# adaLN's four later vectors in a fused encoder layer: from scaled additions over rows of inputs to multiply-and-sum over rows of features, spread over units 7 to 103

## The chip, the cores and the metric

One NeuronCore of a Trainium2 chip runs the whole layer. The metric is the device time of one execution in microseconds, the median of several runs. Engines are named as in the profile: PE multiplies matrices, PEld loads its weights, DVE (VectorE) and ACT (ScalarE) work element by element and read PSUM, POOL (GpSimd) works on SBUF alone, and SP issues nearly all DMAs, in the order of its queue.

## What is computed

Batch 1, 1024 tokens, width 1024, all in fp32. The part that the change concerns is the modulation, six vectors of 1024 from the conditioning vector c:

```python
c_act = jax.nn.silu(c)
mod = c_act @ w_ada + b_ada          # (1, 6*1024), w_ada is 1024 x 6144
shift_mix, scale_mix, gate_mix, shift_ffn, scale_ffn, gate_ffn = jnp.split(mod, N_MOD, axis=-1)

h = modulate(rms_norm(x), shift_mix, scale_mix)
proj = h @ w_in                      # q, k, v of 8 + 8 heads
...                                  # chunked attention, stick-breaking attention
mixed = jnp.concatenate([rms_norm(oa) * g_a, rms_norm(ob) * g_b], axis=-1) @ w_out
x = x + gate_mix[:, None, :] * mixed
h = modulate(rms_norm(x), shift_ffn, scale_ffn)
gate, val = jnp.split(causal_depthwise_conv(h @ w_up, conv_w, conv_b), 2, axis=-1)
x = x + gate_ffn[:, None, :] * ((jax.nn.silu(gate) * val) @ w_down)
return rms_norm(x) * final_g
```

The first two vectors are needed before any projection; the other four only later: `gate_mix` when the output projection is scaled, `shift_ffn` and `scale_ffn` after attention, `gate_ffn` in the feed-forward part.

## The kernel before, in words

Matrix products in fp32 are made of three passes over values split in a high and a low part (`mm3g`), so PE has three matmuls for each product and DVE, ACT and POOL have the splitting.

**Stages.** (1) Norm, the first two modulation vectors and the first head pair's q and k, up to about 70 us of the trace. The two vectors are made here by `ada_sum` (L250): the weights lie with features on partitions, silu(c) is spread over all partitions in the tile `cbc`, and one `tensor_tensor_reduce` (L254) multiplies 1024 inputs and adds them up. (2) Attention, to about 640 us. (3) The rest of the output projection and the second norm. (4) The feed-forward blocks, to the end. The change acts in stage 2.

**Attention.** A loop (L943) runs over 128 units: 8 head pairs of 16 units, the first four pairs stick-breaking (units 0 to 63), the last four chunked attention (units 64 to 127). A pass of the loop computes the scores of the unit two ahead, transposes the weights of the present unit, and multiplies by the values every second unit (`pv`). For a stick-breaking unit the weights need a scan on DVE (L799, tile `kt`), then a product on POOL (L802, tile `pb`), then PE's transposes (`T<-ident,pb`), a copy on ACT (`pth`) and the low part on DVE (`ptl`, L822). For a chunked unit they need a maximum on DVE (L767 to L776, tile `nm`), ACT's exponential (L778, `pb`), and a scaling on POOL (L795). Between these, `fill` deals out a quota of projection matmuls (jobs: q and k of later pairs, v, and at the end `job_out_b`, the first part of the output projection, L545, and `job_out_a`, L581). `job_out_b` loads `gate_mix` into a tile `kt` (L560) and scales its results on DVE (L567, tile `wl`). Its weights are loaded as `raw`, copied on DVE (L521) and POOL (L522) to tiles `H`.

**Order.** PE's instructions are kept in the order in which they are written (`pe`, L135), and so is any instruction wrapped in `ko`. The others, DVE's in attention among them, are placed by a scheduler; SP's DMAs too. Every engine then runs its queue in order: an instruction that waits holds all that stand behind it.

**The four later vectors** (`mods`, L891) are a generator that the loop advances once per unit from unit 60 (`MOD0`, L971). Two tiles of 128 inputs by 256 features (`rawm`, 128 KB, 4 buffers) are handled per step: DVE multiplies each by the input's silu(c) and adds it to a sum `macc` (L916 the first, L918 the other seven of eight). After eight tiles `mod_out` (L923) adds over partitions on PE, with a column of ones (two matmuls `T<-ones,macc`) for `shift_ffn` and `scale_ffn`, or with a matrix of ones (`T<-macc,ones`) for the two gates; DVE adds the bias (L930, L936) and a gate's row goes to DRAM (`gate_d`).

```python
            if kb == 0:
                ...
                acc = mk(p1, [P, QC], F32, "macc")
                ve.tensor_scalar(acc, w, cact[:, 0:1], None, ALU.mult)
            else:
                ve.scalar_tensor_tensor(acc, w, cact[:, kb:kb + 1], acc, ALU.mult, ALU.add)
            if kb == KB - 1:
                mod_out(i, qt, acc, cols)
```

Of the kernel before, what the change touches and what calls it, by code (L numbers as in the profile page):

```python
# [11 lines left out]
F32 = mybir.dt.float32  # L12
F32R = mybir.dt.float32r
AF = mybir.ActivationFunctionType
ALU = mybir.AluOpType
# [4 lines left out]
P = 128  # L20
S = 1024
D = 1024
KB = D // P
TB = S // P
HALF = 512
# [9 lines left out]
NEG = -1.0e30  # L35
# [11 lines left out]
T2A, T2B = 6, 2  # L47
MOD0 = 60
FILL = 2, 2, 0, 0
MODS = 2, 3, 4, 5  # L50
# [5 lines left out]
def build(nc, tc, t, ctx):  # L56
    sy, ve, sc, gp, te = nc.sync, nc.vector, nc.scalar, nc.gpsimd, nc.tensor
    cnt = [0]

    def mk(pool, shape, dt, tag):  # L60
        cnt[0] += 1
        return pool.tile(shape, dt, name=f"{tag}_{cnt[0]}", tag=tag, bufs=BUFS.get(tag, 1))
# [8 lines left out]
    f = lambda ap: ap.bitcast(F32)  # L71


    _, dr = pool("dr", space=DRAM)
# [3 lines left out]
    gate_d = mk(dr, [2, D], F32, "gated")  # L78
    rev_d = mk(dr, [8, P, ULEN], F32, "revd")

    c0, p0 = pool("p0", side="left")
# [12 lines left out]
    bada = sm[:, 16:64]  # L94
# [40 lines left out]
    def pe(fn, *a, **k):  # L135
        r = fn(*a, **k)  # L136
        return tc.keep_in_program_order(r) if pin[0] else r
# [4 lines left out]
    lo64, hi64 = slice(0, HD), slice(HD, P)  # L142
    smask = mk(pq, [P, P], F32, "smask")
    gp.memset(smask, 0.0)
    gp.affine_select(out=smask, in_=smask, pattern=[[-1, P]], compare_op=ALU.is_gt,
                     fill=NEG, base=0, channel_multiplier=1)
    smaskr, identr = (mk(pq, [P, P], F32R, n) for n in ("smaskr", "identr"))
    gp.tensor_copy(smaskr, smask)
    gp.tensor_copy(identr, ident)
# [62 lines left out]
    def new_k(pr):  # L212
        pr.kh = [mk(pq, [P, S], F32R, "kh") for _ in range(2)]
# [3 lines left out]
    cs, pst = pool("pst", side="right", reuse_waits="tile")  # L217
    ada = t["ada0"]
    sh_mix = mk(p0, [P, KB], F32, "sh_mix")
    sc_mix = mk(p0, [P, KB], F32, "sc_mix")  # L220
# [233 lines left out]
    split_v0(1)  # L454
    sy.dma_start(rev_d, bass.AP(t["rev"].tensor, 0, [[ULEN, 8], [0, P], [1, ULEN]]))
    new_k(pairs[0])
    for hf in range(2):
# [84 lines left out]
    def load_gate(dst):  # L542
        sy.dma_start(dst, bass.AP(gate_d.tensor, gate_d.offset, [[0, P], [1, D]]))

    def job_out_b(_):  # L545
# [8 lines left out]
        for fb in fbs:  # L554
            wo[fb, 1] = load_wout(fb, 1)
        bc = mk(p1, [P, S + 1], F32, "kt")
        load_gate(bc[:, 0:D])
        gate.append(bc)
# [329 lines left out]

    QC = 256

    def mods():  # L891


        seq = [(i, qt, kb) for i in MODS for qt in range(D // QC) for kb in range(KB)]
        tiles = {}

        def load(n):
            if n < len(seq):
                i, qt, kb = seq[n]
                tiles[n] = mk(p1, [P, QC], F32, "rawm")  # L900
                sy.dma_start(tiles[n], t["ada"][i - 2, kb, :, qt * QC:(qt + 1) * QC])

        load(0)
        load(1)
        yield
        for n, (i, qt, kb) in enumerate(seq):
            cols = i in (3, 4)
            if n % 2 == 0:
                load(n + 2)
                load(n + 3)  # L910
            w = tiles.pop(n)
            if kb == 0:
                if cols and qt == 0:
                    modv[i] = mk(p0, [P, KB], F32, f"mod{i}")
                acc = mk(p1, [P, QC], F32, "macc")
                ve.tensor_scalar(acc, w, cact[:, 0:1], None, ALU.mult)  # L916
            else:
                ve.scalar_tensor_tensor(acc, w, cact[:, kb:kb + 1], acc, ALU.mult, ALU.add)  # L918
            if kb == KB - 1:
                mod_out(i, qt, acc, cols)  # L920
            if n % 2:
                yield

    def mod_out(i, qt, acc, cols):
        mp = mk(ps1, [P, HALF], F32, "T")
        if cols:
            for b in range(2):
                pe(te.matmul, mp[:, b:b + 1], acc[:, b * P:(b + 1) * P], ones[:, 0:1], start=True, stop=True)
            k0 = 2 * qt
            ve.scalar_tensor_tensor(modv[i][:, k0:k0 + 2], mp[:, 0:2], 0.0 if i == 3 else 1.0,  # L930
                                    bada[:, 8 * i + k0:8 * i + k0 + 2], ALU.add, ALU.add)
        else:
            pe(te.matmul, mp[:, 0:QC], ones, acc, start=True, stop=True)
            bb = mk(p1, [1, QC], F32, "rawm")
            sy.dma_start(bb, bass.AP(t["b_ada"].tensor, i * D + qt * QC, [[QC, 1], [1, QC]]))
            ve.tensor_add(acc[0:1], mp[0:1, 0:QC], bb)  # L936
            sy.dma_start(gate_d[i // 5:i // 5 + 1, qt * QC:(qt + 1) * QC], acc[0:1])

# [5 lines left out]
    for i in range(-AHEAD, len(units) + 1):  # L944
# [23 lines left out]
        for x in later:  # L968
            x[0] -= 1
            if x[0] == 0:  # L970
                x[1]()  # L971
        if i >= MOD0:
            next(bg, None)
# [547 lines left out]
```

## Time and profile before

| | us |
|---|---|
| median of three runs (1423.1 to 1428.0) | 1426.03 |
| the profiled execution | 1425.51 |
| its span, first to last instruction | 1423.5 |
| busy: PE, DVE, POOL, ACT | 1309.2, 1176.2, 864.9, 617.2 |

The span is what the instructions cover; the execution's own time is 2.0 us longer. Busy times are sums over stages that are limited by different things, so a term is read in its stage: the view by stretches gives the busy time of each engine there, the granted clock of PE (1.00 is full speed, 0.5 half) and the DMA share; the view of waits tells who waited for whom.

### The profile page before, as it was taken

How to read it: one execution, taken by the hardware profiler on the slowest of the kernel's cores; microseconds unless marked ns; L12 is line 12 of the kernel's file. 1: busy time of each engine (PE TensorE's matmuls, PEld its weight loads, DVE VectorE, ACT ScalarE, POOL GpSimd, SP SyncE). 2: the span in 40 equal slices, each digit the busy share in tenths (PEclk: the TensorE clock that was granted, in tenths of full speed). 3: DMA queues.
4: the chain of work that ended last, by engine and by line, in shares of the span. 5: the costliest groups of instructions: out<-in, count | busy, mean ns of one | idle time of the engine just before them, and what ended most of it. 6: DMA issues, size and time to landing. Idle time of an engine off the chain costs nothing.

```text
span 1423.5 us, 19845 instructions
## 1 busy us (share of the span) xinstructions
PE 1309.2 (92%) x6644; PEld 1083.0 (76%) x6644; DVE 1176.2 (83%) x1967; ACT 617.2 (43%) x1270; POOL 864.9 (61%) x760
## 2 busy tenths in 40 slices
PE   4889999999899978798887999999999999999996
PEld 2688998898778966676665877777777778777774
DVE  7858777677778868876889889999998889899887
ACT  5647567575545433333432333323333333333334
POOL 4646576765333436563578667776676677667664
PEclk9999999999999999899998999999999999999998
DMA  8534433414665686665011111111111111211213
GB/s 311 180 100 112 104 88 85 119 49 120 166 167 144 179 263 197 217 193 193 22 45 36 47 52 45 45 45 60 52 54 58 45 45 45 60 52 49 62 37 119
DMA packets 80047, 144.57 MB, mean 102 GB/s; under 512 B 10041, under 2 KB 36809, under 8 KB 79946
## 3 DMA queue, kind: packets, MB, share of 16 engines
q1 hardware_dynamic: 79946, 143.31, 33.9%
q8 instruction: 53, 0.87, 0.3%
q14 instruction: 48, 0.39, 0.1%
HBM read 102.89 MB, written 18.88 MB: 86 GB/s over the span
## 4 chain that ended last, share of the span: by engine, by line
PE 43%; DVE 35%; ACT 7%; issue 5%; DMA 5%; POOL 4%; SPq 1%; POOLq 0%; DVEq 0%; ACTq 0%
PE mm L136 14%; PE up L1128 12%; DVE y L1137 8%; PE T L136 6%; PE dnf L136 6%; DVE x L1262 4%; PE S L136 3%; ACT y L1133 3%; DVE ah L1071 3%; DVE y L1070 2%; DVE adaw L254 1%; DVE macc L918 1%; PE up L1302 1%; POOL wl L121 1%; DVE al L1072 1%
## 5 line engine op out<-in xcount | busy, mean ns | idle before, releaser
L1262 DVE TENSOR_TENSOR x<-dnf,x 128x512 f32<-128x512 f32 x340 | 222.5, 679 | 1.6 <-PE dnf L136 1.6
L1137 DVE SCALAR_TENSOR_TENSOR y<-y,sm,y 128x512 f32<-128x512 f32 (+2 forms) x160 | 187.3, 1171 | 28.8 <-ACT y L1133 28.7
L1128 PE MATMUL up<-h,wh 128*128 128x512 f32 x640 | 199.7, 393 | 2.6 <-ACT y L1170 1.8
L1094 POOL TENSOR_TENSOR wl<-raw,wh 128x1024 fp32r<-128x1024 f32 (+1 forms) x62 | 160.1, 2583 | 66.1 <-ACT wh L1092 59.5
L1133 ACT ACTIVATE y<-y,sm 128x512 f32<-128x512 f32 x80 | 65.3, 817 | 254.7 <-DVE y L1209 133.4
L136 PE MATMUL mm<-H,wh 128*128 128x512 f32 x448 | 150.2, 403 | 0.0
L1128 PEld LDWEIGHTS up<-h,wh 128*128 128x128 f32 x640 | 119.7, 189 | 31.1 <-ACT y L1170 5.2
L136 PE MATMUL dnf<-dh,ah 128*128 128x512 f32 x336 | 133.5, 397 | 10.0 <-DVE x L1262 8.8
L136 PE MATMUL dnf<-dl,ah 128*128 128x512 f32 x336 | 134.0, 399 | 3.7 <-POOL dl L1240 2.5
L802 POOL TENSOR_TENSOR pb<-pb,kt 128x512 f32<-128x512 f32 (+2 forms) x96 | 89.4, 945 | 77.0 <-DVE kt L799 50.0
L136 PE MATMUL dnf<-dh,al 128*128 128x512 f32 x336 | 132.6, 395 | 0.9 <-DVE al L1072 0.9
L1128 PE MATMUL up<-h,wl 128*128 128x512 f32 x320 | 125.3, 392 | 0.0
L822 DVE TENSOR_TENSOR ptl<-T,pth 128x512 fp32r<-128x512 f32 (+2 forms) x192 | 98.5, 517 | 30.7 <-ACT pth L821 29.0
L821 ACT CAST pth<-T 128x512 fp32r<-128x512 f32 (+2 forms) x192 | 87.4, 457 | 62.3 <-PE T L136 60.9
L795 POOL TENSOR_SCALAR pb<-pb,ri 128x640 f32<-128x640 f32 (+2 forms) x64 | 45.4, 711 | 106.2 <-DVE ri L794 67.7
L136 PE MATMUL mm<-wh,H 128*128 128x256 f32 x512 | 102.8, 292 | 6.6 <-DVE vs L511 6.6
L799 DVE TENSOR_TENSOR_SCAN kt<-kt 128x128 f32<-128x128 f32 (+3 forms) x64 | 98.2, 1534 | 9.8 <-ACT kt L784 9.4
L1128 PE MATMUL up<-Tc,wh 128*128 128x512 f32 x320 | 100.9, 396 | 4.6 <-ACT y L1154 4.5
L1240 POOL TENSOR_TENSOR dl<-modt,dh 128x512 fp32r<-128x512 f32 x42 | 65.3, 1554 | 64.3 <-ACT dh L1239 64.3
L1237 POOL TENSOR_TENSOR modt<-modt,modt 128x512 f32<-128x512 f32 x44 | 68.8, 1563 | 58.2 <-DMA modt<-w_down 58.2
L136 PE MATMUL S<-kh,qs 128*128 128x384 f32 (+5 forms) x352 | 99.5, 364 | 4.6 <-ACT pb L778 4.4
L136 PE MATMUL T<-ident,pb 128*128 128x128 f32 x528 | 91.1, 277 | 8.8 <-POOL pb L802 3.5
(214 smaller groups left out, 3451.1 us busy)
## 6 DMA issues: line engine op xcount, KB each, us to landing
raw<-w_up SPq DMA_DIRECT2D x44, 512.0 KB, 3.6
rawm<-ada SPq DMA_DIRECT2D x128, 128.0 KB, 2.4
qs<-ex SPq DMA_DIRECT2D x104, 128.0 KB, 2.5
modt<-w_down SPq DMA_DIRECT2D x44, 256.0 KB, 2.7
adaw<-ada SPq DMA_DIRECT2D x16, 512.0 KB, 5.7
raw<-w_qk SPq DMA_DIRECT2D x16, 512.0 KB, 3.6
kh<-ex SPq DMA_DIRECT2D x56, 128.0 KB, 2.6
tbd<-wh SPq DMA_DIRECT2D x18, 256.0 KB, 2.6
```

The lines of the kernel that those rows point to most:

```text
L136: r = fn(*a, **k)
L799: ve.tensor_tensor_scan(r, r, r, 1.0, ALU.mult, ALU.bypass)
L802: gp.tensor_mul(pt[:, a:b], pt[:, a:b], kt[:, a + 1:b + 1])
L821: sc.copy(dh, tp[:, 0:b - a])
L822: ve.tensor_sub(dl, tp[:, 0:b - a], f(dh))
L1094: late.append(lambda a=a, z=z: ko(gp.tensor_sub(wl[:, a:z], raw[:, a:z], f(wh[:, a:z]))))
L1128: ko(te.matmul(ps, w[x][:, kb], b[kb][y], start=start and n == 0, stop=n == 11, skip_group_check=True))
L1133: ko(sc.activation(y[:, a:z], src[:, a:z], AF.Identity, scale=cw[2][:, b], bias=cb[:, b]))
L1137: ko(ve.scalar_tensor_tensor(y[:, o:z], src[:, o - d:z - d], cw[2 - d][:, b], y[:, o:z], ALU.mult, ALU.add))
L1237: ko(gp.tensor_mul(raw, raw, gbc[hf]))
L1240: ko(gp.tensor_sub(wl, raw, f(wh)))
L1262: r = ve.tensor_add(xc, ps, xc)
```

## The change

The four later vectors are made the way `ada_sum` makes the first two. The host hands over the weights transposed, features on partitions. silu(c), which stage 1 has spread over the partitions, is saved in DRAM (`c_d`) and read back spread over 128 partitions, half of it (512 inputs) at a time, into `chalf`. One `tensor_tensor_reduce` on DVE (`ISA rawm,asum` and a second instruction that reads the accumulator) handles 128 features by 512 inputs (`rawm`, now 256 KB, 2 buffers). There are 64 of them: 2 halves, 4 vectors, 8 blocks. They are pinned in order (`ko`). The sum is complete without PE; two small DVE operations add the halves and the bias; a gate is written to DRAM from 128 partitions, element by element. The generator now starts at unit 7 (the first from 6 on that is no multiple of 3) and moves one tile a step, in two units of three, so that the last sum is written at unit 103. `job_out_b` and `job_out_a` are as before, but `job_out_b` first makes sure that the first gate has been issued. The mask `smask` moves to a pool that is closed after stage 1.

```diff
-    "pb": 3, ..., "rawm": 4, ...
+    "pb": 3, ..., "rawm": 2, ...
-MOD0 = 60
+MOD0 = 6
+    c_d = mk(dr, [1, D], F32, "cd")
     sy.dma_start(rev_d, bass.AP(t["rev"].tensor, 0, [[ULEN, 8], [0, P], [1, ULEN]]))
+    sy.dma_start(c_d, cbc[0:1])
         bc = mk(p1, [P, S + 1], F32, "kt")
+        while not gate_up:
+            next(bg)
         load_gate(bc[:, 0:D])
-    QC = 256
+    asum = mk(p0, [P, 2, len(MODS), KB], F32, "asum")
+    gate_up = []
     def mods():
-        seq = [(i, qt, kb) for i in MODS for qt in range(D // QC) for kb in range(KB)]
...
+        seq = [(hf, n, kb) for hf in range(2) for n in range(len(MODS)) for kb in range(KB)]
+        tiles, ch = {}, {}
+        def load(x):
+            if x < len(seq):
+                hf, n, kb = seq[x]
+                cc = slice(hf * HALF, (hf + 1) * HALF)
+                if n == 0 and kb == 0:
+                    ch[hf] = mk(p1, [P, HALF], F32, "chalf")
+                    sy.dma_start(ch[hf], bass.AP(c_d.tensor, c_d.offset + hf * HALF, [[0, P], [1, HALF]]))
+                tiles[x] = mk(p1, [P, HALF], F32, "rawm")
+                sy.dma_start(tiles[x], t["ada"][n, kb, :, cc])
         load(0)
-        load(1)
         yield
...
+        for x, (hf, n, kb) in enumerate(seq):
+            load(x + 1)
+            w = tiles.pop(x)
+            ko(ve.tensor_tensor_reduce(out=w, in0=w, in1=ch[hf], scale=1.0, scalar=0.0, op0=ALU.mult, op1=ALU.add,
+                                       accum_out=asum[:, hf, n, kb:kb + 1]))
+            if hf and kb == KB - 1:
+                mod_out(n, MODS[n])
+            yield
+    def mod_out(n, i):
+        v = modv[i] = mk(p0, [P, KB], F32, f"mod{i}")
+        ve.tensor_add(v, asum[:, 0, n], asum[:, 1, n])
+        ve.scalar_tensor_tensor(v, v, 1.0 if i == 4 else 0.0, bada[:, 8 * i:8 * i + KB], ALU.add, ALU.add)
+        if i in (2, 5):
+            sy.dma_start(bass.AP(gate_d.tensor, gate_d.offset + i // 5 * D, [[1, P], [P, KB]]), v)
+            gate_up.append(i)
-        if i >= MOD0:
+        if i >= MOD0 and i % 3:
             next(bg, None)
-    ada = w6[:, :, 2:6].transpose(2, 0, 1, 3)
+    ada = w_ada[0].T.reshape(6, KB, P, D)[2:6]
```

What it does to the queues, at three places. Line numbers of the changed program are 1 to 4 off those of before (L803 is L799, L826 is L822, L851 is L847, L523 is L521).

DVE in the large units of the first stick-breaking pair, before (`kt` the scans, `ptl` the low parts, `ex` a projection's low part):

```order
L847 TENSOR_TENSOR o_1244<-T_1246,fx_1245 64x256
L822 TENSOR_TENSOR ptl_1264<-T_1261,pth_1263 128x128
L822 TENSOR_TENSOR ptl_1228<-T_1279,pth_1227 128x4x128
L799 SCALAR_TENSOR_TENSOR kt_1271<-kt_1271 128x1024
L160 SCALAR_TENSOR_TENSOR ex_1299<-mm_1146,ex_1298 128x512
L822 TENSOR_TENSOR ptl_1264<-T_1314,pth_1263 128x2x128
L822 TENSOR_TENSOR ptl_1339<-T_1333,pth_1338 128x4x128
```

and after:

```order
L851 TENSOR_TENSOR o_1254<-T_1256,fx_1255 64x256
L826 TENSOR_TENSOR ptl_1274<-T_1271,pth_1273 128x128
L917 ISA rawm_1180,asum_581<-rawm_1180,chalf_1099 128x512
L917 ISA asum_581 128x1
L826 TENSOR_TENSOR ptl_1238<-T_1292,pth_1237 128x4x128
L803 SCALAR_TENSOR_TENSOR kt_1284<-kt_1284 128x1024
L156 SCALAR_TENSOR_TENSOR ex_1312<-mm_1153,ex_1311 128x512
L826 TENSOR_TENSOR ptl_1274<-T_1327,pth_1273 128x2x128
L917 ISA rawm_1277,asum_581<-rawm_1277,chalf_1099 128x512
L917 ISA asum_581 128x1
L826 TENSOR_TENSOR ptl_1355<-T_1349,pth_1354 128x4x128
```

Two sums stand where none stood, each ahead of a low part that PE's value products read. 35 of the 64 sums stand ahead of the last stick-breaking scan, and all 64 ahead of the instructions that the trace of before shows from 505 us on.

DVE near the end of attention, while `job_out_b` runs, before:

```order
L521 CAST H_7672<-raw_7670 128x512
L918 SCALAR_TENSOR_TENSOR macc_7483<-rawm_7598,cact_76,macc_7483 128x256
L793 TENSOR_TENSOR rs_7609<-rs_7609 128x1
L847 TENSOR_TENSOR o_7530<-T_7688,fx_7687 64x256
L794 RECIPROCAL ri_7633<-rs_7609 128x1
L521 CAST H_7678<-raw_7676 128x512
L822 TENSOR_TENSOR ptl_7711<-T_7708,pth_7710 128x128
L855 SCALAR_TENSOR_TENSOR otl_7700<-o_7530,sm_74,oth_7699 128x256
L918 SCALAR_TENSOR_TENSOR macc_7483<-rawm_7600,cact_76,macc_7483 128x256
L764 MEMSET S_7726 64x64
```

and after:

```order
L523 CAST H_7448<-raw_7446 128x512
L797 TENSOR_TENSOR rs_7379<-rs_7379 128x1
L851 TENSOR_TENSOR o_7312<-T_7458,fx_7457 64x256
L798 RECIPROCAL ri_7403<-rs_7379 128x1
L826 TENSOR_TENSOR ptl_7481<-T_7478,pth_7480 128x128
L768 MEMSET S_7484 64x64
L859 SCALAR_TENSOR_TENSOR otl_7470<-o_7312,sm_75,oth_7469 128x256
```

The two additions to `macc` are gone, and nothing of the later vectors stands here any more.

PE at the same place, before:

```order
L136 MATMUL T_7688<-ptl_7511,vs_5290 128x128
L136 MATMUL T_7708<-ident_65,pb_7489 128x128
L136 MATMUL T_7720<-macc_7483,ones_70 128x256
L136 MATMUL S_7726<-kh_6270,vs_6714 128x384 x2
L136 MATMUL mm_7682<-H_6785,H_6768 128x512
```

and after:

```order
L137 MATMUL T_7458<-ptl_7293,vs_5285 128x128
L137 MATMUL T_7478<-ident_66,pb_7271 128x128
L137 MATMUL S_7484<-kh_6187,vs_6587 128x384 x2
L137 MATMUL mm_7452<-H_6658,H_6641 128x512
```

The matmul on `macc` is gone from between a transpose and the scores. There were 24 such matmuls (8 for the gates, 16 for the two columns) and none is left; PE's order is otherwise the same. On SP 128 loads of `rawm`, 8 of the bias and 8 gate rows become 64 loads, two of `chalf`, one write of `c_d` and two gates.

## Rows read from the trace of the kernel before

**Rows 1.** The page: busy time by engine, share of the span, instructions.
```profile
PE 1309.2 (92%) x6644; PEld 1083.0 (76%) x6644; DVE 1176.2 (83%) x1967; ACT 617.2 (43%) x1270; POOL 864.9 (61%) x760
```

**Rows 2.** Stretches of attention: length, busy us (instructions) by engine, clock, DMA share, GB/s.
```profile
core 0: us, PE busy (x) PEld busy (x) DVE busy (x) ACT busy (x) POOL busy (x), PEclk, DMA share, GB/s
100.00:340.00 240.00, 234.82 (x1542) 212.25 (x1542) 180.66 (x257) 159.01 (x377) 162.54 (x227) 0.99 0.37 94
340.00:505.00 165.00, 156.21 (x994) 139.18 (x993) 133.34 (x446) 84.44 (x242) 62.11 (x89) 0.98 0.60 164
505.00:640.00 135.00, 110.53 (x578) 90.08 (x577) 107.33 (x281) 45.02 (x133) 74.31 (x76) 0.92 0.70 216
```

**Rows 3.** The same stretches, instructions on the tile macc alone (PE, PEld, DVE).
```profile
340.00:505.00 165.00, 5.76 (x32) 4.45 (x32) 43.81 (x84) 0.98 0.60 164
505.00:640.00 135.00, 4.71 (x16) 2.70 (x16) 29.64 (x44) 0.92 0.70 216
```

**Rows 4.** PE's waits from 345 to 480 us: total, times, longest.
```profile
PE S L136 <- ACT pb L778: 4.4, 4, 2.3
PE T L136 <- DVE macc L918: 3.1, 1, 3.1
```

**Rows 5.** PE's waits from 480 to 630 us.
```profile
PE T L136 <- DVE macc L918: 8.8, 2, 6.6
PE mm L136 <- DVE H L521: 6.1, 2, 3.6
PE S L136 <- ACT pb L778: 2.2, 1, 2.2
```

**Rows 6.** PE in order of time: start, duration, instruction, idle before.
```profile
343.20 0.65 PE L136 MATMUL T<-macc,ones 128*128 128x256 f32 x2
343.50 0.58 PE L136 MATMUL S<-kh,qs 128*128 128x256 f32 x2
...
600.31 1.19 PE L136 MATMUL T<-macc,ones 128*128 128x256 f32 x2 [6.59 <-DVE macc L918]
```

**Rows 7.** DVE in order of time, 593 to 601 us.
```profile
598.69 1.48 DVE L918 SCALAR_TENSOR_TENSOR macc<-rawm,cact,macc 128x256 f32<-128x256 f32 x1
```

**Rows 8.** Stretches that hold the waits on macc, columns as in rows 2.
```profile
405.00:420.00 15.00, 11.95 (x60) 9.95 (x59) 9.34 (x30) 4.90 (x16) 2.82 (x5) 0.89 0.67 178
545.00:560.00 15.00, 9.88 (x54) 7.57 (x53) 13.22 (x36) 4.20 (x15) 8.58 (x12) 0.97 0.69 226
595.00:610.00 15.00, 9.69 (x47) 8.33 (x48) 11.08 (x26) 2.97 (x8) 7.28 (x7) 0.77 0.52 164
```

**Rows 9.** Groups by line on DVE: count, ns min/median/max; then busy, mean ns, idle.
```profile
L254 DVE CUSTOM_DVE_ANT_0 adaw<-adaw,cbc x16: 1209/1212/2309, 18.2 to 55.4; 128x1024 f32<-128x1024 f32 x16
L771 DVE CUSTOM_DVE_ANT_0 S<-S,kt x64: 285/432/433, 332.9 to 626.8; 128x256 f32<-128x256 f32 x56, 128x128 f32<-128x128 f32 x8
L254 DVE DVE_READ_ACCUMULATOR2_ANT sh_mix<- x8: 76/78/83, 19.3 to 55.0; 128x1 f32 x8
L918 DVE SCALAR_TENSOR_TENSOR macc<-rawm,cact,macc x112: 414/485/1594, 76.9 to 620.0; 128x256 f32<-128x256 f32 x112
...
L918 DVE SCALAR_TENSOR_TENSOR macc<-rawm,cact,macc 128x256 f32<-128x256 f32 x112 | 66.9, 597 | 9.0 <-DMA rawm<-ada 8.0
```

**Rows 10.** Fullest stretches of DVE in stick-breaking, columns as in rows 2.
```profile
130.00:140.00 10.00, 10.00 (x62) 8.70 (x61) 9.02 (x10) 7.90 (x18) 5.58 (x10) 1.00 0.52 124
240.00:250.00 10.00, 10.00 (x64) 8.92 (x64) 9.01 (x11) 8.21 (x20) 8.50 (x12) 1.00 0.36 83
```

**Rows 11.** PE's waits from 70 to 345 us.
```profile
PE T L136 <- POOL pb L802: 3.5, 3, 1.6
PE T L136 <- DVE ptl L822: 1.7, 1, 1.7
```

**Rows 12.** DMA issues by line: count, KB each, median us to landing.
```profile
modt<-w_down SPq DMA_DIRECT2D x44, 256.0 KB, 2.7
```

More of the change, by code (lines that the diff above doesn't have):

```diff
@@ L142, in build @@
     lo64, hi64 = slice(0, HD), slice(HD, P)
[L143 to L146, printed above, removed]
     smaskr, identr = (mk(pq, [P, P], F32R, n) for n in ("smaskr", "identr"))
-    gp.tensor_copy(smaskr, smask)
     gp.tensor_copy(identr, ident)
@@ L218, in build @@
     ada = t["ada0"]
+    smask = mk(pst, [P, P], F32, "smask")
+    gp.memset(smask, 0.0)
+    gp.affine_select(out=smask, in_=smask, pattern=[[-1, P]], compare_op=ALU.is_gt,
+                     fill=NEG, base=0, channel_multiplier=1)
+    gp.tensor_copy(smaskr, smask)
     sh_mix = mk(p0, [P, KB], F32, "sh_mix")
@@ L887, in build @@
     modv = {}
-    QC = 256
+    asum = mk(p0, [P, 2, len(MODS), KB], F32, "asum")
+    gate_up = []
     def mods():
-        seq = [(i, qt, kb) for i in MODS for qt in range(D // QC) for kb in range(KB)]
[L895 to L901, printed above, removed]
+        seq = [(hf, n, kb) for hf in range(2) for n in range(len(MODS)) for kb in range(KB)]
[9 more added lines that the diff above has]
+                sy.dma_start(tiles[x], t["ada"][n, kb, :, cc])
@@ L903, in mods @@
         load(0)
-        load(1)
         yield
[L906 to L937, printed above, removed]
+        for x, (hf, n, kb) in enumerate(seq):
[6 more added lines that the diff above has]
+            yield
```

2 rows, old and new, of the table BUFS are left out of this document.

## The prediction

> **What bounds the kernel now.** I read the page first, then the attention stage in stretches, then PE's waits there, then PE and DVE in order of time at the longest of them. The page says that PE is busy for 92% of the span and DVE for 83% [rows 1]. That alone would make any work taken from either look useful, so the stage decides. In the stretches [rows 2] the reader is to see two regimes. From 100 to 340 us (stick-breaking) PE is busy 234.8 of 240 us: PE bounds, and DVE has 59.3 us to spare. From 340 to 640 us (chunked attention with the output projection) PE is idle for 8.8 us of 165 and then for 24.5 us of 135, its granted clock falls to 0.98 and 0.92, and DVE is busy for 133 of 165 and 107 of 135. There PE waits for others. Instructions on `macc`, the sum that the change replaces, take 43.8 and 29.6 us of DVE in these two stretches [rows 3]: all of the later vectors' cost lies where PE is not full.
>
> PE's waits name it directly: 3.1 us in one wait [rows 4] and 8.8 us in two [rows 5] end with `DVE macc`. The longest shows how: PE stands for 6.59 us before the matmul on `macc` [rows 6], because the last addition stands in DVE's queue behind half a dozen others and itself takes 1.48 us [rows 7], three times its shortest 414 ns [rows 9].
>
> **The change, part by part.** The sum is made against the profiled execution's own 1425.5 us; the median of the three runs is 0.5 us above it, and that is added at the end.
>
> *PE loses 24 matmuls*, in 16 places. At one place the matmul on `macc` starts at 343.20 and the next one at 343.50 [rows 6], 0.30 us, so 16 x 0.30 = 4.8 us. Their busy time of 10.5 us [rows 3] is an upper end, for it overlaps with neighbours. PE's order is fixed, so each is time on PE wherever PE does not wait anyway. I take **-5**.
>
> *PE's waits on `macc` end*: 3.1 + 8.8 = 11.9 us [rows 4, 5]. What is late next is the score matmul and the projection matmul behind it; they need a free score tile and `H` tiles that DVE casts, and DVE's queue there keeps those. Between nothing and 11.9 I take **-9**, since with the longest wait an addition of 1.48 us ahead of those casts goes as well.
>
> *The clock.* In the three stretches that hold these waits the granted clock is 0.89, 0.97 and 0.77 [rows 8]: for a part of each PE ran at 1.2 instead of 2.4 GHz. At full clock they would give back at most 15 x 0.11 + 15 x 0.03 + 15 x 0.23 = 5.6 us, and nothing if other gaps close by bring the same. I take **-3**, half.
>
> *Other waits that DVE feeds.* ACT's exponentials (4.4 and 2.2 us of PE's waits, fed by DVE's maxima) and the casts of output weights (6.1 us) make 12.7 us [rows 4, 5]. One sum of 512 columns costs, by the rows: 1212 ns for 1024 columns and 432 ns for 256 [rows 9] are 1.016 ns a column, which puts 512 at 0.69 us; reading the accumulator adds 0.08; and the mean of the `macc` additions stands 0.18 us above their shortest [rows 9], which I add for the same company: 0.95 us. (Ends: 0.77 alone, and 1.40 if every one were stretched like the longest of L254, 2309 against 1212.) 29 sums fall between 340 and 505 us: 27.6 us, against 43.8 removed, so DVE goes from 133 to 117 of 165. Behind 505 us 29.6 go and nothing comes: 107 to 78 of 135. Between 0 and 12.7 I take **-4**: a third, since POOL, ACT and the transfers in these chains stay.
>
> *What comes in the stick-breaking stage.* 35 sums of 0.95 us are 33 us on DVE, in a stretch where it has 59.3 us idle [rows 2] and PE no room at all. The cover is DVE's idle time, and it is not even. In its fullest stretches DVE is busy 9.0 of 10 us [rows 10]; one sum in 6.9 us (240 / 35) adds 1.4 there, 0.4 too many in each. That is the lower end, some 1 us in all; the upper end is all 33. Behind each sum in DVE's queue stand a scan, which POOL and then PE's transposes wait for, or a low part, which PE's value products wait for. PE's waits on those two are 3.5 and 1.7 us now [rows 11], so most of these chains arrive in time. I take **+5**, nearer to the lower end, for the same reason.
>
> *The rest together.* The loads move the same 16.8 MB in 64 pieces of 256 KB, for which the nearest row lands in 2.7 us [rows 12]. Each is asked for a step ahead, a unit or more, and attention's 128 units take some 4.4 us each (570 us / 128), so I cost them at nothing; if that cover fails, see the third rival. Two gates written element by element, one save of c and two loads of `chalf` lie far from anyone who waits. The move of the mask costs nothing: POOL makes it before attention.
>
> Sum: -5 - 9 - 3 - 4 + 5 = -16, so 1425.5 - 16 = 1409.5, and with the 0.5 us **1410 us**.
>
> **The rivals.** A difference within 0.3% (4.3 us) can't be told from none.
>
> *First, slower: the sums and POOL stand in each other's way in stick-breaking.* The sums read both inputs from SBUF, and POOL is busy 162.5 of 240 us there [rows 2] with products of two SBUF tiles. One of the sixteen sums of L254 took 2309 ns instead of 1212, and an addition to `macc` up to 1594 instead of 414 [rows 9], so two engines do stretch each other. If a sum's full 0.95 us then reaches PE each time, because scan, POOL product and transposes are one chain, all 33 us are on the path: 1425.5 - 21 + 33 + 0.5 = 1438. It decides from 21 / 35 = 0.6 us lost per sum; PE's waits on `pb` and `ptl` from 100 to 340 us would then show over 20 us. Against it: those waits are 5.2 us now although the scans (longer than any sum) meet POOL already. Chance 0.09. The Trainium skill, "SBUF — State Buffer", section "Who interferes with whom", says that a VectorE instruction with two SBUF inputs and a GpSimd instruction that reads SBUF exclude each other, and the one that comes second is fully blocked until the first has finished. The trace agrees with the lock in the single 2309 ns, but also shows a median of 1212 ns, at which it did not bite. By that rule at its worst the change is this rival; by the median row it is the +5 above.
>
> *Second, the waits only change their name.* If the tiles `H` or the exponentials are late where `macc` was, only the matmuls (5) and a third of the direct waits (4) come back, less the 5 of stick-breaking: 1425.5 - 4 + 0.5 = 1422. For it speaks that PE's other waits in the last stretch are as long as those on `macc` [rows 5], against it that DVE loses over a quarter of its work there [rows 3]. Chance 0.08.
>
> *Third, the loads come late.* Before, DVE idled 8.0 us for `rawm` with up to four buffers in hand [rows 9]; now there are two larger ones, and a load waits in SP's queue behind others. If every fourth sum waits a whole landing, 16 x 2.7 = 43 us of DVE, and half of that reaches PE, the gain of 16 is gone and a little more: 1425.5 - 16 + 21.5 + 0.5 = 1431.5; with a quarter reaching it, 1421. I put the case at 1426. Chance 0.05.
>
> *Fourth, all comes back*: 4.8 + 11.9 + 5.6 + 12.7 = 35 less 1 in stick-breaking: 1425.5 - 34 + 0.5 = 1392. Chance 0.12.
>
> **How the numbers follow.** The forecast, 1400 to 1420, has 0.66. With the fourth rival, faster by over 0.3% gets 0.78; the second and third, no change, 0.13; the first, slower, 0.09. The range reaches from the fourth rival's 1392 to 1424, which takes in the second and leaves out the first, half of the third, and a little below: some 0.15.
>
> **What would show it.** Right: no wait of PE on sums after 340 us; the stretch that corresponds to 505 to 640 us shorter by over 10 us, with a clock above 0.95; the sums at 0.69 to 0.75 us in the middle of their durations; stick-breaking longer by at most 10 us, with new waits on `pb` and `ptl`. Wrong: stick-breaking longer by over 20 us (first rival), PE's waits on `H` and `pb` after 340 us grown by what those on `macc` lost (second), DVE idle for `rawm` by tens of us (third), or the middle of the sums' durations near 1.4 us.

## The result, and the profile after

The change takes **1407.3 us** (median of four runs, 1405.0 to 1412.3) against 1425.9 us: ratio 0.988, 95% interval [0.986, 0.990]. That is faster, as forecast, and 2.7 us below the forecast 1410; the profiled execution went from 1425.5 to 1407.9 us, by 17.6. The rest of this document is about where these 17.6 us come from, for it is not where the prediction put them.

The page of the change: VectorE loses 15 us, PE 6, and POOL, which the change gives nothing to do, gains 18 [rows 1].

```profile
PE 1303.2 (93%) x6596; PEld 1074.3 (76%) x6596; DVE 1161.6 (83%) x1959; ACT 616.4 (44%) x1270; POOL 883.0 (63%) x760
```

PE's 6596 instructions that do not touch `macc` come in the same order in both kernels. So the same places can be found in both traces by counting PE's instructions, and the start of one after minus its start before says how far the change is behind (+) or ahead (-) there: -1.3 us at 100, +9.4 at 340, +2.8 at 505, -15.8 at 640, -17.7 at the end (times of before). The stretches of after that hold the work of [rows 2] are therefore these (columns as there):

```profile
98.72:349.46 250.74, 238.80 (x1542) 213.35 (x1541) 211.54 (x333) 159.00 (x377) 180.61 (x227) 0.98 0.48 131
349.46:507.95 158.49, 151.03 (x962) 134.20 (x962) 116.67 (x413) 84.55 (x243) 63.23 (x89) 0.98 0.53 146
507.95:624.22 116.27, 103.69 (x562) 85.07 (x560) 83.39 (x238) 44.33 (x133) 72.64 (x76) 0.96 0.67 207
```

Stick-breaking takes 250.7 us instead of 240 (+10.7), the next stretch 158.5 instead of 165 (-6.5), the last 116.3 instead of 134.9 (-18.6); all that follows gives 1.9. In the first, VectorE is busier by the sums, and POOL by 18 us with the same instructions: something stretches them. In the last, PE's idle time falls from 24.5 to 12.6 us and the clock rises from 0.92 to 0.96.

The sums themselves by line (count, ns min/median/max; then busy, mean):

```profile
L917 DVE CUSTOM_DVE_ANT_0 rawm<-rawm,chalf x64: 664/687/1614, 118.8 to 507.0; 128x512 f32<-128x512 f32 x64
L917 DVE DVE_READ_ACCUMULATOR2_ANT asum<- x64: 72/77/84, 119.7 to 507.6; 128x1 f32 x64
  DMA rawm<-ada: 2.6, 1
```

The estimate of 0.69 alone and 0.08 for reading holds. Of the 64 sums 37 fall in stick-breaking and 27 behind it (the prediction had 35 and 29). VectorE waited for a load once, 2.6 us. PE's waits in stick-breaking, against 3.5 and 1.7 us [rows 11]:

```profile
PE T L137 <- POOL pb L806: 5.9, 3, 2.6
PE T L137 <- DVE ptl L826: 3.2, 4, 1.3
PE T L137 <- DVE ri L798: 2.3, 1, 2.3
```

And behind it, from 349 to 624 us, where the waits on `macc` (11.9 us in three [rows 4, 5]) are gone and no name has taken their place; the largest growth is that of `ptl`, from 1.9 to 4.7 us:

```profile
PE S L137 <- ACT pb L782: 5.3, 6, 1.6
PE T L137 <- DVE ptl L826: 4.7, 6, 1.8
PE mm L137 <- DVE H L523: 4.2, 3, 1.6
PE mm L137 <- POOL H L524: 2.0, 3, 0.8
```

### The profile page after: what moved, and what is told of

It reads as the page before. It is cut to its first block, busy times and chain, and to the rows that moved or that the text cites. A ratio compares the mean times of both kernels' runs of the same rounds, so it can differ in the third digit from the quotient of the medians.

```text
span 1405.9 us, 19550 instructions
## 1 busy us (share of the span) xinstructions
PE 1303.2 (93%) x6596; PEld 1074.3 (76%) x6596; DVE 1161.6 (83%) x1959; ACT 616.4 (44%) x1270; POOL 883.0 (63%) x760
## 4 chain that ended last, share of the span: by engine, by line
PE 40%; DVE 37%; ACT 7%; POOL 6%; issue 5%; DMA 4%; SPq 0%; POOLq 0%; DVEq 0%; ACTq 0%
PE mm L137 13%; PE up L1121 12%; DVE y L1130 9%; PE T L137 6%; PE dnf L137 5%; DVE x L1255 4%; ACT y L1126 3%; PE S L137 3%; DVE ah L1064 3%; DVE y L1063 2%; POOL pb L806 2%; POOL wl L122 1%; DVE adaw L255 1%; DVE al L1065 1%; DVE kt L803 1%
## 5 line engine op out<-in xcount | busy, mean ns | idle before, releaser
L806 POOL TENSOR_TENSOR pb<-pb,kt 128x512 f32<-128x512 f32 (+2 forms) x96 | 102.1, 1077 | 68.4 <-DVE kt L803 45.1
L137 PE MATMUL dnf<-dh,ah 128*128 128x512 f32 x336 | 133.0, 396 | 11.6 <-DVE x L1255 10.1
L826 DVE TENSOR_TENSOR ptl<-T,pth 128x512 fp32r<-128x512 f32 (+2 forms) x192 | 98.4, 515 | 21.7 <-ACT pth L825 20.0
L799 POOL TENSOR_SCALAR pb<-pb,ri 128x640 f32<-128x640 f32 (+2 forms) x64 | 46.1, 721 | 102.7 <-DVE ri L798 62.0
L803 DVE TENSOR_TENSOR_SCAN kt<-kt 128x128 f32<-128x128 f32 (+3 forms) x64 | 97.1, 1517 | 6.1 <-ACT kt L788 5.2
```

The costliest lines, as they stand in the source:

```text
L803: ve.tensor_tensor_scan(r, r, r, 1.0, ALU.mult, ALU.bypass)
L806: gp.tensor_mul(pt[:, a:b], pt[:, a:b], kt[:, a + 1:b + 1])
L826: ve.tensor_sub(dl, tp[:, 0:b - a], f(dh))
```

## The experiments

Twelve kernels, each timed beside the kernel before (1424.5 to 1425.8 us). Most leave the later vectors out or compute something else in their place. The table gives how much longer (+) or shorter (-) each took in the three stretches than the kernel before, by PE's instructions as above, and how many sums (or what stands for them) start there. These come from one profile each; the medians in the text are the times. The -2 to -3 in the first column is a gap of the kernel before at 335 us: up to 330 us those runs are within 0.3 us of it.

```
                                  100-340        340-505        505-640     sums in the three
the change                         +10.7           -6.5          -18.6       37 27  0
no sums, no loads                   -2.9          -17.8          -21.1        0  0  0
loads, no consumer                 +24.8          -18.1          -21.0        0  0  0
loads, one-column copy              -2.8          -13.7          -16.7       37 27  0
sums, one load only                +10.1           -8.6          -19.0       37 27  0
one-input reduction, 512            -2.2           -6.3          -17.5       37 27  0
one-input reductions, 512 + 384     +4.5           -5.7          -15.3       37 27  0
before, no PE matmuls              +55.5          -16.6          -20.2      all before 307 us
before, one-column additions        +0.1           -3.9          -10.4        as before
sums from unit 60                   -0.1           -7.0           +0.3        3 39 22
sums in every unit                 +36.6          -14.2          -19.6       57  7  0
two sums a unit before unit 6      +22.2          -11.9          -21.5       46 11  0
as many, in shorter units          +10.9           -7.9          -17.3       37 27  0
```

**1. What do all the later vectors cost?** Neither sums nor loads (the later vectors are not computed):

```diff
-                tiles[x] = mk(p1, [P, HALF], F32, "rawm")
-                sy.dma_start(tiles[x], t["ada"][n, kb, :, cc])
+                tiles[x] = None
-            ko(ve.tensor_tensor_reduce(out=w, in0=w, in1=ch[hf], ...
```

> The changed kernel without any of the 64 sums and without their loads (the four vectors are then only bias; two gates are still written). Theory (the sums cost some 11 us in stick-breaking, through DVE, and nothing much later): about 1396, and stick-breaking back at the length of before, PE's waits on pb and ptl from 100 to 350 us at 5 us or less. Rival (stick-breaking is longer for another reason, such as the moved mask, the saved c or another order of PE): within 3 us of the changed kernel's 1407.

Measured: 1381.3 us, ratio 0.970 [0.968, 0.971], 15 us less than expected. The loss in stick-breaking is gone, as it should be, but the stretches behind it give 39 us, not 25. So what the change leaves there costs another 14 us, which the prediction put nowhere, and all that the later vectors still cost in the change is 26 us. (The saves of the two gates move to 71 us in this run, where nobody waits: it is level with the kernel before at 100 us. So it has no save in the stretches of the table, which experiments 2 and 5 make use of.)

**2. Loads or sums?** Loads without the sums, and sums with one load only:

```diff
 f_loads
-            ko(ve.tensor_tensor_reduce(out=w, in0=w, in1=ch[hf], ...
 f_sums
-                tiles[x] = mk(p1, [P, HALF], F32, "rawm")
-                sy.dma_start(tiles[x], t["ada"][n, kb, :, cc])
+                if x == 0:
+                    tiles[-1] = mk(p1, [P, HALF], F32, "rawm")
+                    junk.append(mk(p1, [P, HALF], F32, "rawm"))
+                    sy.dma_start(tiles[-1], t["ada"][n, kb, :, cc])
+                tiles[x] = tiles[-1]
```

> The changed kernel with all 64 loads but no sum (the four vectors are then only bias). Theory (DVE's time is the cost): as without both, about 1396, at most 2 us above it. Rival (the loads are the cost, by SP's queue or DMA traffic in stick-breaking): about 1405 to 1407.

> The changed kernel with all 64 sums but one load: all sums read the same tile and write their products to a second one (the four vectors are wrong). Theory (DVE): as the changed kernel, about 1407, at least 1404. Rival (the loads): about 1397.

Measured: loads only 1409.0, 0.990 [0.988, 0.991]; sums only 1404.0, 0.986 [0.984, 0.987]. The second is clear: with no loads the whole loss in stick-breaking stays (+10.1). The first is a miss that teaches something else. With nobody to wait for them the loads were all brought forward, to between 72 and 213 us, and SP's queue in order of time shows what stood in it (start, duration, out<-in, count):

```profile
106.79 13.56 SPq L911 DMA_DIRECT2D rawm<-ada  x10
121.10 2.64 SPq L911 DMA_DIRECT2D rawm<-ada  x2
125.35 4.80 SPq L911 DMA_DIRECT2D rawm<-ada  x4
131.14 0.50 SPq L174 DMA_DIRECT2D kh<-ex  x1
```

The load of the keys `kh` came behind 16 of them, and PE waited once for all of it:

```profile
PE T L137 <- DVE ptl L826: 17.3, 1, 17.3
```

So loads without a consumer are not the loads of the change. The next run gives them one that costs next to nothing:

```diff
+            ko(ve.tensor_copy(asum[:, hf, n, kb:kb + 1], w[:, 0:1]))
```

> All 64 loads at the pace of the change, but each sum is replaced by a copy of one column (under 0.1 us), so the later vectors are not computed. If the loads cost nothing, the time is that of the run with neither sums nor loads, 1381, up to 1385, and no wait of 17 us stands at 110 to 150 us. If the loads as such disturb (SyncE's queue, memory traffic), it is 1390 or more.

Measured: 1392.2, 0.977 [0.975, 0.979], the second case. In stick-breaking, though, the loads cost nothing (-2.8, as without them), and the long wait is gone. Behind it 27 loads and copies, and the two saves of the gates, which stand there again, cost 8 us (30.4 against 38.9). Of these 8.5 us, 6.4 are lost in the 30 us from the issue of the two saves (2.7 and 3.7, counted along PE against the run without sums and loads); what is left for the loads and copies is some 2. So the prediction's "nothing" for the loads holds in the first stretch, and nearly so behind it. The costs do not add up: sums without loads give 27.6 us behind 340, 11 less than the run with neither, and sums with loads 25.1. The saves stand behind 340 us in the run with sums, in the run with loads and copies and in the change alike, so that 11 and 8 make 14 and not 20.

**3. VectorE's time, or a shared way into SBUF?** The sum is replaced by a plain reduction of the same tile, which has one SBUF input instead of two; then by two such reductions, so that VectorE has more to do than in the change:

```diff
 f_onein
-            ko(ve.tensor_tensor_reduce(out=w, in0=w, in1=ch[hf], ...
+            ko(ve.tensor_reduce(asum[:, hf, n, kb:kb + 1], w, AX.X, ALU.add))
 f_onein2 (beside it)
+            ko(ve.tensor_reduce(asum[:, hf, n, kb:kb + 1], w[:, 0:384], AX.X, ALU.add))
```

> The changed kernel with each sum made by a plain reduction of the 512 columns, with one input from SBUF instead of two, and without the accumulator's reading (the product with silu(c) is left out). If the 11 us come from two inputs on the ports that POOL uses too: the mean of these instructions near their median (0.55 to 0.70 us, the sums have 0.69 and 0.86), and about 1398 to 1401. If they come from DVE's time alone: in proportion to its busy time, (0.93 - 0.65) / 0.93 of 11 us = 3 us less, about 1404.

> Each sum of 512 products is replaced by two plain reductions with one SBUF input, of 512 and of 384 columns (the first took 671 ns, the second should take some 0.5 us): VectorE is then busy for some 1.2 us a step, longer than the 0.93 us of the sum and its reading, and the later vectors are not computed. If stick-breaking is longer because VectorE has more to do, this run loses there as much as the change or more: at 330 us TensorE stands 8 to 13 us behind the kernel before, and the time is 1405 to 1410. If it is longer because the sum's two SBUF inputs and GpSimd's products keep each other out, this run loses nothing there (0 to 2 us at 330 us), GpSimd's 128x512 products stay at 1.15 to 1.19 us, and the time is about 1396 to 1399.

Measured: one reduction 1395.3, 0.979 [0.978, 0.981], below both cases; two 1404.8, 0.985 [0.983, 0.987]. The time of the second stands at the edge of its first case, and its 4.5 us in stick-breaking lie between the two, so neither case holds alone. The durations of the two:

```profile
L917 DVE TENSOR_REDUCE asum<-rawm x64: 648/672/687, 120.2 to 503.0; 128x1 f32<-128x512 f32 x64
L918 DVE TENSOR_REDUCE asum<-rawm x64: 486/543/554, 121.5 to 504.3; 128x1 f32<-128x384 f32 x64
```

1.2 us of VectorE a step, against 0.99 (0.913 and 0.077) for the sums of the change in stick-breaking, and yet that stretch loses 4.5 us instead of 10.7; with 0.67 us a step it loses nothing. None of the 128 reductions took over 0.69 us, while a sum took up to 1.61. POOL's products of two SBUF tiles, from 100 to 350 us, in the change and with two reductions (count | busy, mean ns | idle):

```profile
L806 POOL TENSOR_TENSOR pb<-pb,kt 128x512 f32<-128x512 f32 x48 | 61.2, 1281 | 46.5 <-DVE kt L803 30.0 <-PE T L137 4.5 <-ACT kt L788 3.7
```

```profile
L806 POOL TENSOR_TENSOR pb<-pb,kt 128x512 f32<-128x512 f32 x48 | 54.4, 1140 | 62.8 <-DVE kt L803 40.7 <-PE T L137 5.1 <-PE S L137 4.3
```

1140 ns is the mean of the kernel before too (1142; 1178 with one reduction). One meeting in the change, VectorE first and then POOL:

```profile
206.10 0.66 DVE L826 TENSOR_TENSOR ptl<-T,pth 128x512 fp32r<-128x512 f32 x1
206.68 1.61 DVE L917 CUSTOM_DVE_ANT_0 rawm<-rawm,chalf 128x512 f32<-128x512 f32 x1
208.22 0.08 DVE L917 DVE_READ_ACCUMULATOR2_ANT asum<- 128x1 f32 x1
208.22 1.30 DVE L803 TENSOR_TENSOR_SCAN kt<-kt 128x128 f32<-128x128 f32 x1
```

```profile
206.66 2.59 POOL L806 TENSOR_TENSOR pb<-pb,kt 128x512 f32<-128x512 f32 x2
```

The sum starts 20 ns after a product of 1.09 us and takes 1.61 us, about that product's time and a sum's own; POOL's next product, which started within the sum, takes 1.54 instead of 1.09. Over all sums in stick-breaking, the 32 that overlap with an instruction of POOL take 950 ns in the mean, the 5 that do not 677; for the one-input reductions it is 671 and 674. A sum also writes 512 columns where a reduction writes one. A row of the change itself speaks against this as the cause: 46 of the 48 large low parts, which read one tile of PSUM and one of SBUF and write 512 columns, overlap with a TENSOR_TENSOR of POOL, and none took over 0.70 us (count | busy, mean ns | idle):

```profile
L826 DVE TENSOR_TENSOR ptl<-T,pth 128x512 fp32r<-128x512 f32 x48 | 32.6, 680 | 12.9 <-ACT pth L825 12.5
```

So the first rival's mechanism is real, at a price of its own: plain VectorE time is some 4 us at most of the 10.7, and the rest is put down to POOL and VectorE keeping each other out where an input pair meets. The Trainium skill, "SBUF — State Buffer", section "Who interferes with whom", says that two SBUF inputs on VectorE contend with a GpSimd instruction that reads SBUF. It says too that an instruction with at most one does not, as long as it is outside the two-port performance modes, which casts can enter. The runs agree on the sums and the reductions, and show that the condition matters: the casts of output weights, with one SBUF input, take 400 ns at the shortest and up to 1508, at 541.96 us, 50 ns after a 1.28 us difference of two SBUF tiles has started on POOL:

```profile
L523 DVE CAST H<-raw x16: 400/416/1508, 516.4 to 613.1; 128x512 fp32r<-128x512 f32 x16
```

Behind 340 us the rule decides nothing: there one-input reductions cost as much as the sums (-6.3 and -17.5 against -6.5 and -18.6).

**4. What did the matmuls and the additions of before cost?** The kernel before without the 24 matmuls, and then with additions of one column:

```diff
 b_nomm
-        mp = mk(ps1, [P, HALF], F32, "T")
+        mp = acc
-                pe(te.matmul, mp[:, b:b + 1], acc[:, b * P:(b + 1) * P], ones[:, 0:1], start=True, stop=True)
-            pe(te.matmul, mp[:, 0:QC], ones, acc, start=True, stop=True)
 b_short
-                ve.scalar_tensor_tensor(acc, w, cact[:, kb:kb + 1], acc, ALU.mult, ALU.add)
+                ve.scalar_tensor_tensor(acc[:, 0:1], w[:, 0:1], cact[:, kb:kb + 1], acc[:, 0:1], ALU.mult, ALU.add)
```

> The kernel before without the 24 matmuls that finish the later vectors on TensorE (the result is then wrong for these vectors); additions and loads stay. By the prediction, which put 5 us on the matmuls themselves, 9 on TensorE's waits for the sums and 3 on the clock, this takes 1407 to 1412. If the second half is limited by VectorE's load rather than by these waits, the waits move on to the next name and it takes 1416 to 1422.

> The kernel before with each of the 112 additions cut from 256 columns to one, so the later vectors are not computed; loads, the order of the work, the 24 matmuls on TensorE and the first product of each sum stay. It stands beside the run with loads and a one-column copy and no matmuls (1392.2): the difference is the price of the 24 matmuls with what is left of their waits. If they cost what the prediction put on them, 5 us, this takes 1396 to 1399, and the additions as VectorE's load cost the kernel before some 28 us. If the matmuls are most of the gain, it takes 1405 or more. If they cost nothing, 1392.

Measured: without matmuls 1441.0, **slower**, 1.012 [1.010, 1.013]; with one-column additions 1409.3, 0.989 [0.987, 0.991]. The first misses both bands and is no test of what it was made for. The matmuls were what held the additions in their place: PE's order is fixed, VectorE's additions are not. Without them all 112 run between 77 and 307 us, beside POOL's products (mean 597 ns before [rows 9], 656 now), and PE waits:

```profile
L918 DVE SCALAR_TENSOR_TENSOR macc<-rawm,cact,macc 128x256 f32<-128x256 f32 x112 | 73.4, 656 | 13.9 <-DMA rawm<-ada 11.7
```

```profile
PE T L136 <- DVE ptl L822: 21.7, 19, 2.8
```

That costs 55 us in stick-breaking, and 37 of them come back behind it. The second keeps the order: cutting VectorE's additions short gives 15 us, and what remains (the loads, the matmuls, the 16 first products, the eight saves and 112 additions of 219 ns in the median) still costs 28 (1409.3 against 1381.3). By its number this is the case in which the matmuls are most of the gain, but how much of these 28 is the matmuls was not separated: here 117 of the 128 half-size loads are issued behind 340 us, in the run with copies 25 of 64.

**5. Form or place?** The change with its place undone, and the place pushed further:

```diff
 g_late
-MOD0 = 6
+MOD0 = 60
-        if i >= MOD0 and i % 3:
+        if i >= MOD0:
 h_all
-        if i >= MOD0 and i % 3:
+        if i >= MOD0:
```

> The change with its placement undone: one sum in every unit from 60 on, so all 64 lie behind stick-breaking. There must be no loss at 330 us (0 to 1 us). If each sum costs the same 0.45 us behind stick-breaking as the 29 of the change do there, 1426 - 43 + 64 x 0.45 = 1412. If the cost grows with how full VectorE is, 1416 or more; if the sums cost less where GpSimd is less busy, 1405 or less.

> The change with a sum in every unit from 6 on instead of two in three: 58 of the 64 lie in stick-breaking. If a sum costs 0.3 us there whatever their number, and 0.45 behind it, 1426 - 43 + 58 x 0.3 + 6 x 0.45 = 1403, with TensorE some 17 us late at 340 us. If the cost of one grows as VectorE fills (in the run without the matmuls, additions of 73 us in the same stretch cost 52 us, 0.7 us for each us of work), 57 x 0.93 x 0.7 = 37 us are lost there and the time is 1418 to 1423.

Measured: sums from unit 60 on 1423.9, ratio 0.9995 [0.998, 1.001]; in every unit from 6 on 1420.0, 0.997 [0.996, 0.999]. Both fall into the slower of the cases that were named, the first 12 us above the 1412 of equal cost: **the new form at the old place gives nothing that can be measured.** Followed along PE, however, this kernel is 10 us ahead of the kernel before at 495 us (times of before), 2.6 behind at 530, 9 ahead again at 629 and 1 ahead at 650. It loses 12 and 8 us in two steps. At both the same DMA has just been issued, the save of an output gate, 4 KB, element by element (L929). SP's queue at the first:

```profile
484.95 0.38 SPq L929 DMA_DIRECT2D gated<-mod  x1
485.81 0.34 SPq L910 DMA_DIRECT2D rawm<-ada  x1
486.25 0.38 SPq L568 DMA_DIRECT2D wh<-x  x1
486.73 0.47 SPq L174 DMA_DIRECT2D kh<-ex  x1
```

Before, during and behind it, in the stretches of all engines (the last two columns are the DMA share and GB/s):

```profile
480.00:486.00 6.00, 6.00 (x32) 5.04 (x31) 4.94 (x16) 2.39 (x6) 2.40 (x4) 1.00 0.60 151
486.00:497.00 11.00, 9.54 (x55) 8.12 (x54) 5.85 (x20) 4.12 (x12) 1.14 (x2) 1.00 0.67 35
497.00:503.00 6.00, 4.20 (x24) 3.31 (x22) 0.99 (x4) 0.00 (x0) 0.81 (x1) 1.00 0.99 214
```

For 11 us the DMA engines are busy for 0.67 of the time and move 35 GB/s; the loads issued behind the save land 14 to 15 us later. The chain that ended last goes through one of them:

```profile
487.89 15.07 DMA kh<-ex
503.02 6.19 DMA H<-otld
```

PE then waits from 485 to 530 us for these and what hangs on them:

```profile
PE mm L137 <- DVE H L523: 9.1, 2, 5.2
PE T L137 <- DVE nm L778: 4.4, 1, 4.4
```

The kernel before saved its gates in eight rows of 1 KB. With a sum in every unit, stick-breaking loses 36.6 us, 0.64 for each of 57, against 0.29 for each of 37 in the change, and 10 to 13 of it at one place, the first save again (issued at 294.30); without these it is 0.41 to 0.47 a sum. The stretches of that kernel, and VectorE:

```profile
290.00:297.00 7.00, 7.00 (x44) 6.03 (x43) 6.93 (x15) 3.06 (x9) 5.05 (x8) 1.00 0.70 145
297.00:306.00 9.00, 6.60 (x36) 5.33 (x35) 1.24 (x3) 2.93 (x8) 2.49 (x4) 1.00 0.24 13
306.00:312.00 6.00, 0.00 (x0) 0.00 (x0) 0.58 (x1) 0.00 (x0) 0.00 (x0) 0.51 0.87 250
```

```profile
298.52 0.69 DVE L803 TENSOR_TENSOR_SCAN kt<-kt 128x256 f32<-128x256 f32 x1
311.42 0.69 DVE L917 CUSTOM_DVE_ANT_0 rawm<-rawm,chalf 128x512 f32<-128x512 f32 x1 [12.20 <-DMA rawm<-ada]
```

The sum waits 12.2 us for its load, all that is pinned behind it on VectorE waits as well, and PE stands still for 6 us. The change has the two saves at 366 and 509 us. Its DMA issues from 366 to 380 us, and those of the same work in the run without sums and loads, 352 to 366 us there (KB each, median us to landing; `rawm` takes 3.0 us over the whole kernel):

```profile
rawm<-ada SPq DMA_DIRECT2D x2, 256.0 KB, 11.5
kh<-ex SPq DMA_DIRECT2D x4, 128.0 KB, 11.3
```

```profile
kh<-ex SPq DMA_DIRECT2D x4, 128.0 KB, 3.0
```

So the loads are late there too, and PE pays for it. Against the kernel before this is hard to see, since that one loses time of its own soon after. Against the run without sums and loads, the time lost along PE in the 30 us from the issue of each save is

```
                                  first save    second save
the change                            4.1            2.1
loads, one-column copy                2.7            3.7
sums from unit 60                    12.4            6.6
sums in every unit                   13.1            1.1
two sums a unit before unit 6         1.0            2.9
```

and in the change it does not come back: it is 14.4 us behind that run until 378 us, 19.6 at 400, 23.8 from 500 to 515 and 26.3 at 550. So some 6 us of the 14 that the prediction put nowhere stand at the two saves. All lines but the second hold the cost of the sums in these 30 us as well, so they are upper ends.

What the two runs show of place is therefore of two kinds: sums cost more where more of them stand beside full engines, and the saves move with the sums. Without what is lost at the saves, the run with sums from unit 60 would not end at -4.4 us (in the profiled execution) but at about -23, and the change not at -17.7 but at about -24. By this estimate the 64 sums cost much the same at both places, and the change is faster than that run mostly because its saves hold up less. A version that saves the gate in long rows was not tried, so this is not shown.

**6. A better place?** Two sums a unit before unit 6, where VectorE is busy for 10 of 30 us; and as many sums in stick-breaking as in the change, beside the shorter scans only:

```diff
 h_early
+        if i < MOD0:
+            next(bg, None)
+            next(bg, None)
 h_short_units
-        if i >= MOD0 and i % 3:
+        if i >= MOD0 and ((i + 3) % 16 < 11 if i < 64 else i % 3):
```

> The change, with two sums in each of the eight units ahead of unit 6 as well, 16 sums in all, in the 30 us at the start of attention where VectorE is busy for 10 of 30 us and TensorE for 24; the rest follow at the pace of the change and so end earlier, about unit 78 instead of 102. If a sum costs where GpSimd's products and VectorE's chain are full (0.3 us each in stick-breaking, 0.4 behind it), some 16 x 0.4 = 6 us come back: 1400 to 1403. If the early sums delay the first units instead (their loads are late, or they stand ahead of the first scans), it is 1407 or more.

> The change with as many sums in stick-breaking (the rest is placed as in the change), but not in two of every three units: in each round of 16 units they stand, one a unit, beside the eleven shorter scans (128 to 768 columns), and none beside the last five, whose scans have up to 1024 columns. VectorE and GpSimd are fullest beside those. If a sum costs by how full these two are at its place, TensorE is 3 to 6 us behind the kernel before at 330 us instead of 8.5, and the time is 1401 to 1404. If the lock takes its price wherever a sum falls, it stays at 8 to 10 us and 1406 to 1408. If one sum a unit is too fast for its load, VectorE waits for loads by over 10 us in stick-breaking, and it is 1410 or more.

Measured: 1410.9, 0.990 [0.988, 0.992], and 1409.7, 0.991 [0.989, 0.992]; neither beats the change. The early sums put the kernel 5 us behind by 110 us, and stick-breaking with nine sums more than in the change loses 22. Beside shorter scans the loss is the same, 10.9 us; POOL is stretched less (173.5 us busy in stick-breaking against 180.6), and VectorE waited 10.4 us for loads, four times as long as in the change, so fuller places avoided and later loads may have cancelled. This run does not tell the two apart.

## Why the prediction was right, and where it was not

*Result.* The sign, the range and the time are right; the sum of -16 was -17.6 in the profiled execution, made of -25 behind 340 us (predicted -21), +10.7 in stick-breaking (predicted +5), and -3.2 before and after. Two terms were off by 4 to 6 us in opposite directions, so that the time came out closer than its parts is luck.

*PE's matmuls (-5), its waits on `macc` (-9), the clock (-3).* The waits went and no other name took their place; the clock behind 505 us rose from 0.92 to 0.96. The three were not measured one by one: the run without the matmuls moved the additions, and the one with short additions bounds matmuls, loads and first products together (28 us). The second rival, waits that only change their name, did not come in the change. With the form alone at the old place the time was the second rival's, by another mechanism, the saves.

*Other waits (-4).* VectorE's 117 of 165 us was right (116.7 of 158.5). The step's flaw is that it gave what stays no price: against the run without sums and loads it is 14 us, some 6 of them at the saves of the gates. The stretches gave 25 us all the same, more than the -21 of all four terms.

*Stick-breaking (+5, ends 1 and 33).* The mechanism was named, the size was half: +10.7, 0.29 us a sum. That it took the size "nearer to the lower end" was argued from VectorE's idle time and from PE's short waits on these chains. Experiment 3 shows that more VectorE time (1.2 us) costs less than half of it; what counts is that sums and POOL's products stretch each other, POOL by 139 ns a 128x512 product. The first rival's mechanism (chance 0.09) acted, but at 0.29 us a sum, not at the 0.95 us that make its 1438, and below the 0.6 from which it decides.

*Loads at nothing.* Right in stick-breaking. Behind it 27 loads with copies and the two saves cost 8 us when the sums are away, of which some 2 are left for the loads.

*The gates at nothing.* "Two gates written element by element ... lie far from anyone who waits" is the step that failed without showing in the time. It looked at who waits for the gate, and not at who stands behind it in the DMA queues. The loads behind the save land after 11 to 15 us, and PE loses 4 and 2 us at the two saves of the change, up to 13 with the sums elsewhere.

*Signs that were named.* No PE wait on sums behind 340: so. The last stretch shorter by over 10 us with a clock above 0.95: 18.6, 0.96. Sums at 0.69 to 0.75 in the middle: 0.687, the lower end. Longer waits on `pb` and `ptl`: 9.1 against 5.2 us. Stick-breaking longer by at most 10: 10.7, just missed.

## What to carry to other kernels

Background work has a price by its place: 0.29 us a sum at two in three units, 0.41 to 0.47 at one a unit (0.64 with the save that moved there), in a stretch that had 59 us of VectorE to spare; so its pace is worth a run of its own. An operation that is put beside another engine's work is chosen by what it reads as well as by how long it takes. And a small DMA is costed by what is queued behind it, not by who waits for its data; when an experiment takes out a consumer or moves a producer, look first where the rest went.

## What the runs showed of the hardware that was not expected

A save of 4 KB in 1024 pieces of 4 bytes took 11.6 us (both times in the kernel with a sum in every unit). In some nine of them, from 297 to 306 us, the DMA engines moved 13 GB/s instead of 145, and the keys' loads issued behind it landed after 15 us:

```profile
gated<-mod SPq DMA_DIRECT2D x2, 4.0 KB, 11.6
```

And two engines that meet on two-input work do not share: a sum of 0.69 us took 1.61 and a product of 1.09 us 1.54, while 128 one-input reductions beside the same products never took over 0.69. One input is not enough by itself, though: a cast of 0.40 us took 1.51.
